# Eight raw weight buffers, two buffers for the modulation's rows, and a root taken in columns

## The chip, the cores and the metric

The kernel runs on one core of a Trainium2 chip. The metric is the device time of one execution, in microseconds (us); before the change it is 2404.76 us, the median of three runs (2402.72 to 2405.74). Lower is better.

The core has engines that run beside each other, each through its own queue of instructions in order: TensorE (PE in the profile; its weight loads are listed as PEld), VectorE (DVE), ScalarE (ACT), GpSimd (POOL) and SyncE (SP). Here SP issues nearly all transfers. Work on data goes on in SBUF, an on-chip memory of 128 partitions; matmuls write to PSUM, a second one.

## The reference

One layer of a decoder trunk over 256 tokens of width 2048, all in float32, and a last norm:

```
mods = (silu(c) @ ada_w + ada_b).reshape(9, 2048)      # modulation: 9 vectors of 2048
h = rms_norm(x, ffn1_norm) * (1 + mods[1]) + mods[0]
x = x + 0.5 * mods[2] * (silu(h @ w_gate) * (h @ w_up)) @ w_down        # first FFN, width 5632
h = rms_norm(x, mix_norm) * (1 + mods[4]) + mods[3]
x = x + mods[5] * mixer(h)      # gated delta rule (8 heads) beside sparse attention (8 heads), gates, w_out
h = rms_norm(x, ffn2_norm) * (1 + mods[7]) + mods[6]
x = x + 0.5 * mods[8] * second_ffn(h)
y = rms_norm(x, final_norm)
```

Nearly all bytes are weights, each read once: 564 MB come from HBM, 151 MB of them the modulation's matrix `ada_w` (2048 x 18432).

## The kernel before, in words

Activations lie transposed: 16 tiles of 128 channels by 256 tokens. A float32 product is made of two parts that TensorE takes in its float32r form: each weight tile is split into a rounded part (`whi`, ScalarE, L186 or L357) and the rest (`wlo`, VectorE, L187 or L358), the activations likewise (`hpair`, `apair`). `product` (L192) runs `whi` against both activation parts (512 columns) and `wlo` against the first (256 columns).

**Weights.** `wload` (L172) fetches a projection's weights in tiles of 512 KB, 4 KB a partition, into buffers of the name `raw`: there are `RB = 6` of them, shared by everything that is loaded under this name. `wsplit` (L181) splits each into one of `WB = 3` pairs of `whi` and `wlo`; a raw buffer is free when `wlo` is written. A projection over 2048 channels (`proj`, L201) has two such tiles and 16 x 2 matmuls, a down-projection of an FFN three tiles and 22 x 2. `block_load` and `block_rows` (L344, L353) do the same for four channel tiles and a gate and up column tile at once.

**Modulation.** The matrix `ada_w` is not multiplied on TensorE. `ada_cols` (L236) loads the 128 rows of one output tile in two halves, each 512 KB, also into `raw` buffers (then called `adaraw`), and VectorE reduces each against `silu(c)` (L248, 1.28 us) into a column of `modc`. A reduction isn't issued at once: it goes to the list `late`, and `behind` (L162) lets it out behind a later `wlo` subtraction, one or two at a time, held to that place in VectorE's order. `ada(n)` (L265) takes n output tiles, two loads each, from a queue; `pace` and `paces` (L332, L545) spread them: 16 over the first 22 projections of the gate and up stage, 32 over the next 42 projections, and in the mixer 4 over 27, 20 over 20 and 24 over 36.

**Order.** The program fixes what depends on what; a planner orders each engine's instructions when the program is built, by its own estimate of when each is ready, and gives buffers out as they come free. On the chip each queue then runs strictly in that order.

**Stages.** The first FFN opens with `start` (L426). The modulation's first two vectors are not there yet, so the first 22 of 44 gate and up tiles are summed in four quarters of the channels, while the rows for the next quarter are loaded and reduced. Before the first quarter, `start` needs the norm's root: 16 matmuls of `ones` against the squares (L432) leave the sum of squares of each token in all 128 partitions, 256 columns wide; the root (`rsqrt`, L273: one start value and three rounds of three VectorE steps) is taken on that tile of 128 x 256, issued when the mods' loop stands at `KT - 5`. After `start` come the other 22 tiles (`gate_up`, L503), with `down(0)` between and `down(1)` after them (L521). Then the mixer: delta rule in four groups of two heads with the compression of keys and values beside it, attention in two groups, the merge (`merge_gates`, L1088, ten tiles ahead of the up-projections), `w_out`; then the second FFN and the last norm.

**Small buffers.** In the mixer each temporary has a name and a number of buffers. The norms after the first one take their root in columns: `token_sums` (L296) makes a 128 x 2 tile, `inv_rms` (L302) takes the root of it and spreads it over the partitions with two matmuls.

Of the kernel before, what the change touches and what calls it, by code (L numbers as in the profile page):

```python
# [18 lines left out]
F32 = mybir.dt.float32  # L19
# [3 lines left out]
AF = mybir.ActivationFunctionType  # L23
OP = mybir.AluOpType
# [3 lines left out]
P = 128  # L28
S = 256
D = 2048  # L30
KT = D // P
FF = 5632
FT = FF // P
NG = 2
GF = FT // NG
AB = 33
H = 8
WB = 3
RB = 6
TB = 6  # L40
MM = 3
NS = 22
SIZES = ((4,), (4,), (4,), (4,))
# [9 lines left out]
EPS = 1e-6  # L53
# [51 lines left out]
def trunk(tc, a, out, stage=99, dbg=None):  # L105
    nc = tc.nc
    ctx = ExitStack()
    with ctx:
# [4 lines left out]

        def ptile(shape=(P, 512), dt=F32, tag="c", bufs=7 - MM):
            return psum.tile(list(shape), dt, tag=tag, name=tag, bufs=bufs)
# [14 lines left out]
        ones = cf[:, C_ONE:C_ONE + P]  # L130
        ident_r = cr[:, 0]
        V = {}
# [101 lines left out]
        ada_q = []  # L234

        def ada_cols(m, d, now=False):  # L236

            part = [V["ada_b"][:, m * KT + d:m * KT + d + 1]]
            for hf in range(2):
                raw = wp.tile([P, HC], F32, tag="raw", name="adaraw", bufs=RB)  # L240
                nc.sync.dma_start(raw, a["ada_w"][m * KT + d, :, hf * HC:(hf + 1) * HC])

                def sums(hf=hf, raw=raw):
                    if hf == 0:
                        out_ = nrm.tile([P, 1], F32, tag="part", name="part", bufs=2)
                    else:
                        out_ = modc[:, m, d:d + 1]
                    nc.vector.tensor_tensor_reduce(out=raw, in0=raw, in1=cact[:, hf * HC:(hf + 1) * HC], scale=1.0,  # L248
                                                   scalar=part[0], op0=OP.mult, op1=OP.add, accum_out=out_)
                    part[0] = out_  # L250

                late.append(sums)
                if now:
                    flush()
                yield
# [170 lines left out]
        def start(fp, n, sizes, wgu, gain):  # L426
            A = nrm.tile([P, KT], F32, tag="A", name="A", bufs=2)
            pt = ptile((P, S))
            for d in range(KT):
                sq = tmp()  # L430
                nc.scalar.activation(sq, xT[:, d], AF.Square)
                nc.tensor.matmul(pt, ones, sq, start=(d == 0), stop=(d == KT - 1))  # L432
            hT = []
            sums = [fp.tile([P, 2, S], F32, tag="a", name="gu", bufs=AB) for _ in range(n - RES)]
            pairs = []
            with tc.tile_pool(name="sp", bufs=1) as sp:
# [41 lines left out]
                for kt, _ in enumerate(mods(*offs[0][0])):  # L478
                    if kt == KT - 5:
                        v = nrm.tile([P, S], F32, tag="ssq", name="vb", bufs=1)  # L480
                        nc.vector.tensor_scalar(v, pt, 1.0 / D, EPS, op0=OP.mult, op1=OP.add)
                        rb = rsqrt(sp, v, "rb")
                for b in range(len(sizes)):
# [13 lines left out]

        def ffn(fp, wgu, wd, m_gate, ticks, first, post=None):
            if True:
# [33 lines left out]

                while len(aT) < AB:
                    aT.append(gate_up(len(aT)))
                down(0)
                while len(aT) < FT:
                    aT.append(gate_up(len(aT)))
                down(1)

# [32 lines left out]
        with tc.tile_pool(name="ffn", bufs=1) as fp:  # L573
            ffn(fp, a["w1gu"], a["w1d"], 2, paces((16 - LT, 2 * (AB - NS)), (32, 42)),
                lambda fp: start(fp, NS, SIZES, a["w1gu"], V["n1"]), post1)
        if stage == 1:
# [9 lines left out]
        with ExitStack() as mx:  # L586
# [14 lines left out]
            def one(tag="q", bufs=12):  # L601
                return mp.tile([P, S], F32, tag=tag, name=tag, bufs=bufs)
# [14 lines left out]

            sm = mp.tile([P, S], F32, name="sm")
            both(win(0), sm)
# [84 lines left out]
            def gdn_group(h0, q, k, v):  # L704
# [113 lines left out]
                for j in range(4):  # L818
                    nc.tensor.transpose(pt[:, j], z[lo, j, lo], ident[lo, lo])
                zq = mp.tile([P, 4, 64], F32, tag="zq", name="zq", bufs=1)  # L820
                nc.scalar.activation(zq[lo], pt, AF.Copy)
# [64 lines left out]
            def gdn_out(h0, oT):  # L886
                for i in range(2):
                    h = h0 + i
                    zg = both(win(W_GZ + h))
                    th = tmp()  # L890
                    nc.scalar.activation(th, zg, AF.Tanh, scale=0.5)
                    sg = mp.tile([P, S], F32, tag="sg", name="sg", bufs=1)
                    nc.vector.scalar_tensor_tensor(sg, th, 1.0, zg, op0=OP.add, op1=OP.mult)
                    sv = sg.rearrange("p (a b) -> p a b", a=2)
                    nc.vector.tensor_mul(sv, sv, v4(oT)[:, :, i])
                    oA[h] = big("oA", 8, (P, 2, S), F32R)
                    split(oA[h], sg)
# [6 lines left out]
            def compress():  # L904
                for b in range(2):
                    cat = mp.tile([P, 2, S], F32, tag="cat", name="cat", bufs=2)
                    for g in range(2):
# [176 lines left out]
            yf = []  # L1084
            mtags = ["kE", "Dt", "N", "o", "vn", "oT", "kd", "kd", "cat", "cat"] + ["pr", "pr", "kk", "kk", "vt", "vt"]
            sgs = []
# [7 lines left out]

            AHEAD = 10
            for d in range(AHEAD):
# [126 lines left out]
```

## Time and profile before

| | |
|---|---|
| median of three runs | 2404.76 us (2402.72 to 2405.74) |
| the profiled execution | 2399.2 us, of which the profile's span is 2397.4 |
| granted TensorE clock, mean | 0.988 of full speed |
| PE, DVE, ACT busy | 96%, 74%, 47% of the span |
| transfers | 571.00 MB, 238 GB/s on the mean |

The page of the profile gives busy time of each engine, the chain of work that ended last (followed back from the last instruction to what released each step), the costliest groups of instructions, and for transfers the time from issue to landing. Other views answer for a stretch: instructions in order of time, busy time and count by windows, the chain in order of time. L187 is line 187 of the kernel. In a row such as `wlo<-raw,whi`, names are those of tiles. Times in a trace start at the span's start.

### The profile page before, as it was taken

The page shows a single profiled execution, that of the slowest core. Times are in us where ns is not written, and L with a number is a line of the kernel's source. Part 1 is how long each engine was busy: PE and PEld are TensorE (multiplying, and loading weights), DVE is VectorE, ACT ScalarE, POOL GpSimd, SP SyncE. Part 2 cuts the span into 40 slices and gives each one's busy share as a digit, 9 for nine tenths or more (in the row PEclk, how much of TensorE's full clock was granted, in tenths as well). Part 3 has the DMA queues.
Part 4 walks back from the last instruction along what each step waited for, and adds up shares of the span by engine and source line. Part 5 has one row for each costly group of instructions (what it writes and reads, how often), then busy time and mean ns, then how long its engine had stood idle before and what let it go on. Part 6 is the DMA issues. An engine that isn't in the chain of part 4 may idle for free.

```text
span 2397.4 us, 38975 instructions
## 1 busy us (share of the span) xinstructions
PE 2301.0 (96%) x15094; PEld 2029.9 (85%) x15094; DVE 1781.4 (74%) x2896; ACT 1133.5 (47%) x1787; POOL 1.4 (0%) x8
## 2 busy tenths in 40 slices
PE   6999999999999999999999999999999999999997
PEld 4999987887778888887778888889888888888886
DVE  6888877777777797778887778879666666555555
ACT  3433544433444474554545444556544444344453
POOL 0000000000000000000000000000000000000000
PEclk8999999999999999999999999999999999999999
DMA  9988678888888745547676888666777777665663
GB/s 320 319 299 301 199 260 286 285 289 286 273 291 268 245 158 188 170 151 249 226 252 214 284 290 283 214 218 216 232 242 243 241 243 219 192 195 189 184 191 123
DMA packets 174493, 571.00 MB, mean 238 GB/s; under 512 B 17890, under 2 KB 18146, under 8 KB 174308
## 3 DMA queue, kind: packets, MB, share of 16 engines
q1 hardware_dynamic: 173584, 566.09, 72.0%
q8 instruction: 118, 1.93, 0.3%
q10 hardware_dynamic: 724, 2.43, 0.3%
q14 instruction: 67, 0.55, 0.1%
HBM read 564.25 MB, written 4.19 MB: 237 GB/s over the span
## 4 chain that ended last, share of the span: by engine, by line
PE 62%; DMA 17%; DVE 12%; ACT 5%; issue 4%; ACTq 0%; DVEq 0%; SPq 0%
PE mm L196 34%; PE mm L198 18%; DMA raw<-in_w1gu_dram 9%; PE mm L363 5%; DVE wlo L187 4%; DMA raw<-in_win_dram 4%; ACT whi L186 3%; DMA raw<-in_w1d_dram 2%; DVE adaraw L248 2%; PE c L363 2%; DVE wlo L358 1%; ACT whi L357 1%; DMA raw<-in_wup_dram 0%; DVE gu L464 0%; PE c L799 0%
## 5 line engine op out<-in xcount | busy, mean ns | idle before, releaser
L196 PE MATMUL mm<-hpair,whi 128*128 128x512 f32 x3536 | 1249.9, 394 | 17.2 <-ACT whi L186 8.9
L187 DVE TENSOR_TENSOR wlo<-raw,whi 128x1024 fp32r<-128x1024 f32 (+1 forms) x666 | 796.5, 1197 | 485.1 <-ACT whi L186 477.0
L186 ACT ACTIVATE whi<-raw 128x1024 fp32r<-128x1024 f32 (+1 forms) x666 | 690.6, 1038 | 800.3 <-PE mm L196 268.3
L198 PE MATMUL mm<-hpair,wlo 128*128 128x256 f32 x3536 | 1009.4, 286 | 20.7 <-DVE wlo L187 20.2
L196 PEld LDWEIGHTS mm<-hpair,whi 128*128 128x128 f32 x3536 | 667.5, 189 | 161.3 <-ACT whi L186 13.3
L198 PEld LDWEIGHTS mm<-hpair,wlo 128*128 128x128 f32 x3536 | 671.7, 190 | 37.4 <-DVE wlo L187 34.8
L196 PE MATMUL mm<-apair,whi 128*128 128x512 f32 x1408 | 490.2, 391 | 0.8 <-ACT whi L186 0.8
L198 PE MATMUL mm<-apair,wlo 128*128 128x256 f32 x1408 | 398.3, 283 | 2.0 <-DVE wlo L187 1.9
L196 PEld LDWEIGHTS mm<-apair,whi 128*128 128x128 f32 x1408 | 265.1, 188 | 56.5 <-ACT whi L186 1.1
L363 PE MATMUL mm<-hpair,whi 128*128 128x256 f32 x1472 | 262.0, 281 | 17.7 <-ACT hpair L323 16.9
L198 PEld LDWEIGHTS mm<-apair,wlo 128*128 128x128 f32 x1408 | 266.8, 190 | 3.7 <-DVE wlo L187 3.6
L363 PEld LDWEIGHTS mm<-hpair,whi 128*128 128x128 f32 x1472 | 226.1, 189 | 18.8 <-ACT hpair L323 17.3
L363 PE MATMUL mm<-hpair,wlo 128*128 128x256 f32 x736 | 208.4, 283 | 6.9 <-DVE wlo L358 6.7
L248 DVE CUSTOM_DVE_ANT_0 adaraw<-adaraw,cact,vec 128x1024 f32<-128x1024 f32 x144 | 184.0, 1278 | 14.0 <-DMA adaraw<-in_ada_w_dram 14.0
L357 ACT ACTIVATE whi<-raw 128x1024 fp32r<-128x1024 f32 x112 | 118.7, 1060 | 155.9 <-DMA raw<-in_w1gu_dram 87.0
L248 DVE CUSTOM_DVE_ANT_0 adaraw<-adaraw,cact,part 128x1024 f32<-128x1024 f32 x144 | 183.9, 1278 | 0.1
L358 DVE TENSOR_TENSOR wlo<-raw,whi 128x1024 fp32r<-128x1024 f32 x112 | 136.3, 1222 | 43.9 <-ACT whi L357 43.5
L363 PEld LDWEIGHTS mm<-hpair,wlo 128*128 128x128 f32 x736 | 138.9, 189 | 10.8 <-DVE wlo L358 10.3
L222 ACT ACTIVATE t<-mm 128x256 f32<-128x256 f32 x237 | 86.7, 367 | 15.5 <-PE mm L198 15.4
L225 DVE TENSOR_TENSOR t<-mm,t 128x256 f32<-128x256 f32 x193 | 80.7, 418 | 4.8 <-ACT t L222 4.7
L529 DVE SCALAR_TENSOR_TENSOR xT<-mm,g,xT 128x256 f32<-128x256 f32 x128 | 61.5, 481 | 7.1 <-PE mm L198 5.4
L514 ACT ACTIVATE t<-t 128x256 f32<-128x256 f32 x63 | 26.0, 413 | 58.2 <-DVE t L225 58.2
(363 smaller groups left out, 1495.4 us busy)
## 6 DMA issues: line engine op xcount, KB each, us to landing
adaraw<-in_ada_w_dram SPq DMA_DIRECT2D x288, 512.0 KB, 5.6
raw<-in_w2gu_dram SPq DMA_DIRECT2D x180, 512.0 KB, 4.7
raw<-in_w1gu_dram SPq DMA_DIRECT2D x176, 512.0 KB, 5.8
raw<-in_win_dram SPq DMA_DIRECT2D x158, 512.0 KB, 4.8
raw<-in_w1d_dram SPq DMA_DIRECT2D x64, 512.0 KB, 5.2
raw<-in_w2d_dram SPq DMA_DIRECT2D x64, 512.0 KB, 3.5
raw<-in_wup_dram SPq DMA_DIRECT2D x32, 512.0 KB, 4.7
raw<-in_wout_dram SPq DMA_DIRECT2D x32, 512.0 KB, 4.6
```

The costliest lines, as they stand in the source:

```text
L186: nc.scalar.activation(hi[:, :n], raw[:, :n], AF.Copy)
L187: behind(nc.vector.tensor_sub(lo[:, :n], raw[:, :n], hi[:, :n]))
L196: nc.tensor.matmul(ps[:, :], hi, pairs[k][:, :, :].rearrange("p a b -> p (a b)"), start=(k == 0), stop=False, skip_group_check=True)
L198: nc.tensor.matmul(ps[:, S:2 * S], lo, pairs[k][:, 0, :], start=False, stop=(k == n - 1), skip_group_check=True)
L222: nc.scalar.activation(t, ps[:, S:2 * S], AF.Copy)
L225: nc.vector.tensor_add(o, ps[:, :S], t)
L248: nc.vector.tensor_tensor_reduce(out=raw, in0=raw, in1=cact[:, hf * HC:(hf + 1) * HC], scale=1.0, scalar=part[0], op0=OP.mult, op1=OP.add, ...
L357: nc.scalar.activation(hi, raw, AF.Copy)
L358: behind(nc.vector.tensor_sub(lo, raw, hi))
L363: nc.tensor.matmul(ps[:, w], l[:, w, k], h[:, r], start=(first and w == k == x == 0), stop=(last and k == kb - 1 and x == 2), skip_group_c ...
L514: nc.scalar.activation(s, g, AF.Silu, bias=bg)
L529: nc.vector.scalar_tensor_tensor(xT[:, d], pd[:, j * S:(j + 1) * S], g05[:, d:d + 1], xT[:, d], op0=OP.mult, op1=OP.add)
```

## The change

`RB` goes from 6 to 8. In the first FFN, once `start` is done, a pool `ring` with `AR = 2` more buffers of the same size is open, and there `ada_cols` takes its buffers from it, so that all eight `raw` buffers go to weights; in `start`, in the mixer and after it the rows still share the `raw` buffers. In `start` the sums of squares are made as columns (the squares are the stationary operand, one column of `ones` the moving one), and the root is taken by `inv_rms`, issued at `KT // 2`, and copied to `rb`. To make room, four temporaries of the mixer take buffers of other names, and the merge's gates lie in other buffers and run eight tiles ahead instead of ten.

```diff
-RB = 6
+RB = 8
 TB = 6
+AR = 2
...
+        own = []
+
+        def ada_tile():
+
+            if own:
+                return own[0].tile([P, HC], F32, tag="ring", name="adaraw", bufs=AR)
+            return wp.tile([P, HC], F32, tag="raw", name="adaraw", bufs=RB)
+
         def ada_cols(m, d, now=False):
...
-                raw = wp.tile([P, HC], F32, tag="raw", name="adaraw", bufs=RB)
+                raw = ada_tile()
...
-            pt = ptile((P, S))
+            pt = ptile()
             for d in range(KT):
                 sq = tmp()
                 nc.scalar.activation(sq, xT[:, d], AF.Square)
-                nc.tensor.matmul(pt, ones, sq, start=(d == 0), stop=(d == KT - 1))
+                for j in range(2):
+                    nc.tensor.matmul(pt[:, j:j + 1], sq[:, j * P:(j + 1) * P], ones[:, 0:1], start=(d == j == 0),
+                                     stop=(d == KT - 1), skip_group_check=True)
...
-                    if kt == KT - 5:
-                        v = nrm.tile([P, S], F32, tag="ssq", name="vb", bufs=1)
-                        nc.vector.tensor_scalar(v, pt, 1.0 / D, EPS, op0=OP.mult, op1=OP.add)
-                        rb = rsqrt(sp, v, "rb")
+                    if kt == KT // 2:
+                        rb = nrm.tile([P, S], F32, tag="ssq", name="rb", bufs=1)
+                        nc.scalar.activation(rb, inv_rms(pt), AF.Copy)
...
-                while len(aT) < AB:
-                    aT.append(gate_up(len(aT)))
-                down(0)
-                while len(aT) < FT:
-                    aT.append(gate_up(len(aT)))
-                down(1)
+                def rest():
+                    while len(aT) < AB:
+                        aT.append(gate_up(len(aT)))
+                    down(0)
+                    while len(aT) < FT:
+                        aT.append(gate_up(len(aT)))
+                    down(1)
+
+                if ring:
+                    with tc.tile_pool(name="ring", bufs=1) as rp:
+                        own.append(rp)
+                        rest()
+                        own.pop()
+                else:
+                    rest()
...
-                lambda fp: start(fp, NS, SIZES, a["w1gu"], V["n1"]), post1)
+                lambda fp: start(fp, NS, SIZES, a["w1gu"], V["n1"]), post1, True)
...
-            sm = mp.tile([P, S], F32, name="sm")
+            sm = one()
...
-                zq = mp.tile([P, 4, 64], F32, tag="zq", name="zq", bufs=1)
+                zq = mp.tile([P, 4, 64], F32, tag="S", name="zq", bufs=1)
...
-                    sg = mp.tile([P, S], F32, tag="sg", name="sg", bufs=1)
+                    sg = mp.tile([P, S], F32, tag="qr", name="sg", bufs=2)
...
-                    cat = mp.tile([P, 2, S], F32, tag="cat", name="cat", bufs=2)
+                    cat = mp.tile([P, 2, S], F32, tag="kk", name="cat", bufs=2)
...
-            mtags = ["kE", "Dt", "N", "o", "vn", "oT", "kd", "kd", "cat", "cat"] + ["pr", "pr", "kk", "kk", "vt", "vt"]
+            mtags = ["kE", "Dt", "N", "o", "vn", "oT", "kd", "kd", "pr", "pr", "kk", "kk", "vt", "vt", "pT", "pT"]
...
-            AHEAD = 10
+            AHEAD = 8
```

More of the change, by code (lines that the diff above doesn't have):

```diff
@@ L495, in start, with ffn @@
             return hT, pairs, ()
-        def ffn(fp, wgu, wd, m_gate, ticks, first, post=None):
+        def ffn(fp, wgu, wd, m_gate, ticks, first, post=None, ring=False):
             if True:
```

## The prediction

> **What bounds the kernel now.** First the page: the busy shares, then the chain that ended last, then the median landing times.
>
> ```profile
> PE 2301.0 (96%) x15094; PEld 2029.9 (85%) x15094; DVE 1781.4 (74%) x2896; ACT 1133.5 (47%) x1787; POOL 1.4 (0%) x8
> ...
> PE 62%; DMA 17%; DVE 12%; ACT 5%; issue 4%; ACTq 0%; DVEq 0%; SPq 0%
> ...
> adaraw<-in_ada_w_dram SPq DMA_DIRECT2D x288, 512.0 KB, 5.6
> ...
> raw<-in_w1gu_dram SPq DMA_DIRECT2D x176, 512.0 KB, 5.8
> ```
>
> PE at 96% looks finished, but matmul ends are modelled and a stretched matmul counts as busy, while 17% of the chain is transfers. So I count matmuls per stretch, in the view by windows.
>
> ```profile
> core 0: us, PE busy (x) PEld busy (x) DVE busy (x) ACT busy (x) POOL busy (x), PEclk, DMA share, GB/s
> 10.00:20.00 10.00, 10.00 (x28) 6.70 (x28) 6.28 (x11) 7.01 (x19) 0.00 (x0) 1.00 1.03 404
> 60.00:240.00 180.00, 171.95 (x1419) 167.27 (x1418) 154.62 (x212) 75.20 (x87) 0.00 (x0) 1.00 0.90 306
> 240.00:300.00 60.00, 60.00 (x517) 60.00 (x516) 49.93 (x77) 35.18 (x62) 0.00 (x0) 1.00 0.62 200
> 300.00:780.00 480.00, 455.86 (x2540) 392.39 (x2540) 361.94 (x518) 202.47 (x273) 0.00 (x0) 0.99 0.84 280
> 1080.00:1320.00 240.00, 225.40 (x1565) 190.81 (x1564) 203.17 (x475) 118.14 (x259) 0.00 (x0) 0.99 0.71 235
> 1320.00:1500.00 180.00, 171.53 (x959) 148.22 (x959) 137.77 (x196) 80.10 (x113) 0.00 (x0) 0.99 0.84 286
> 1740.00:1980.00 240.00, 240.00 (x1387) 212.78 (x1386) 165.01 (x223) 117.07 (x173) 0.00 (x0) 1.00 0.75 243
> ```
>
> The second FFN (1740 to 1980) runs 1387/240 = 5.78 matmuls a us without a hole: a projection of 32 takes 5.54 us. The rest of the first FFN (300 to 780) would make 480 x 5.78 = 2774 and makes 2540: 234 missing, **40.5 us lost**. The merge (1320 to 1500) lacks 81 of 1040, **14.1 us**. The first FFN's opening, in blocks of 256 columns, runs 517/60 = 8.62 when whole; 60 to 240 lacks 132 of 1551, **15.3 us**. The attention stretch (1080 to 1320) has 14.6 us of idle PE. What PE waits for is in the load queue and the chain of waits.
>
> ```profile
> 311.60 4.53 SPq L177 DMA_DIRECT2D raw<-in_w1gu_dram  x4
> 319.01 1.86 SPq L241 DMA_DIRECT2D adaraw<-in_ada_w_dram  x2
> 322.02 1.87 SPq L177 DMA_DIRECT2D raw<-in_w1gu_dram  x2
> 324.70 1.79 SPq L241 DMA_DIRECT2D adaraw<-in_ada_w_dram  x2
> 330.68 1.86 SPq L177 DMA_DIRECT2D raw<-in_w1gu_dram  x2
> 333.69 1.87 SPq L241 DMA_DIRECT2D adaraw<-in_ada_w_dram  x2
> 336.93 0.33 SPq L177 DMA_DIRECT2D raw<-in_w1gu_dram  x1
> ```
> ```profile
> 322.02 6.21 DMA raw<-in_w1gu_dram
> ...
> 328.33 1.07 ACT whi L186
> ...
> 329.43 1.23 DVE wlo L187
> ...
> 330.68 3.79 DMA raw<-in_w1gu_dram
> ```
>
> The loop closes on itself: load 6.21, split 1.07 and 1.23, and only the split's end gives back the buffer for the next load, 8.66 us after the last one (322.02 to 330.68), where PE wants 5.54. A projection with a modulation row takes four of the six buffers. From 311.60 to 336.93 the queue issues 14 tiles for four projections: 25.33 us against 22.2. That is 1.81 us a tile, so each of six buffers turns round in 10.86 us.
>
> **The change, part by part.** *Eight buffers, shared (opening, mixer).* At the same turn-round a tile comes every 10.86/8 = 1.36 us. The mixer's densest stretch, a row at every projection (four tiles), then needs 5.43 us, the merge with 24 rows in 36 projections (3.33 tiles) 4.5: both under 5.54, if the transfers deliver. They did 404 GB/s at 10 to 20 us; the merge at full pace wants 286 x 1040/959 = 310. I take 11 of the merge's 14.1 us (5 to 14), and of the attention's 14.6 idle us, part of which is short dependent work that no buffer shortens, 6 (0 to 12). In the opening VectorE is close behind: 154.62 us busy at 1419 blocks' matmuls is 169 of 180 at 1551. So 5 of 15.3 (0 to 12).
>
> *Two buffers for the modulation's rows (from about 300 us).* Weights alone then have eight buffers at two tiles a projection, four projections deep: their loop is open. The rows get a loop of their own: the reduction ends, the next row half's load is issued, lands, is reduced.
>
> ```profile
> L248 DVE CUSTOM_DVE_ANT_0 adaraw<-adaraw,cact,vec 128x1024 f32<-128x1024 f32 x144 | 184.0, 1278 | 14.0 <-DMA adaraw<-in_ada_w_dram 14.0
> L187 DVE TENSOR_TENSOR wlo<-raw,whi 128x1024 fp32r<-128x1024 f32 (+1 forms) x666 | 796.5, 1197 | 485.1 <-ACT whi L186 477.0
> ...
> L225 DVE TENSOR_TENSOR t<-mm,t 128x256 f32<-128x256 f32 x193 | 80.7, 418 | 4.8 <-ACT t L222 4.7
> ```
>
> 1.28 + 5.6 = 6.9 us against 5.54 where rows follow each other. Each half-row waits in VectorE's order behind a weight subtraction, so a late row holds the next subtraction. `pace` gives runs of three and a pause: two steps of 1.34, 2.7 us late per run. The split may be two tiles ahead (three hi/lo buffers), 5.5 us less its own 1.06 + 1.23: 3.2 us of cover. The pause gives back 5.54 less 2 x 1.23 and two additions of 0.42, 2.2 us. So nearly all is hidden; with that cover gone it is 2.7 us x 11 runs (44 projections), 30 us. The 32 down-projections, longer, give the rows time. I leave a quarter of the 40.5 us for the 0.5 us per run, runs of four and refills: gain 30 (11 to 38). [...]
>
> *The root in columns.* Now the root of a 128x256 tile is woven between the first sixteen reductions, the last three steps after them.
>
> ```profile
> 16.10 1.28 DVE L248 CUSTOM_DVE_ANT_0 adaraw<-adaraw,cact,part 128x1024 f32<-128x1024 f32 x1
> 17.30 0.08 DVE L248 DVE_READ_ACCUMULATOR2_ANT modc<- 128x1 f32 x1
> 17.30 1.28 DVE L248 CUSTOM_DVE_ANT_0 adaraw<-adaraw,cact,part 128x1024 f32<-128x1024 f32 x1
> ...
> 34.42 1.06 ACT L357 ACTIVATE whi<-raw 128x1024 fp32r<-128x1024 f32 x1 [15.06 <-DMA raw<-in_w1gu_dram]
> ...
> 36.81 0.42 DVE L282 SCALAR_TENSOR_TENSOR rby<-rbt,rby 128x256 f32<-128x256 f32 x1
> ...
> 38.44 0.58 PE L363 MATMUL mm<-hpair,whi 128*128 128x256 f32 x1 [16.95 <-ACT hpair L323]
> ```
> ```profile
> 11.51 9.98 PE L432 MATMUL c<-t,cf 128*128 128x256 f32 x32
> ```
> ```profile
> 2384.29 0.61 PE L299 MATMUL c<-cf,ssq 128*128 128x1 f32 x4 [2.00 <-DVE ssq L294]
> ```
> ```profile
> 2384.93 0.16 DVE L305 TENSOR_SCALAR v<-c 128x2 f32<-128x2 f32 x1 [0.70 <-PE c L299]
> ...
> 2386.90 0.16 DVE L282 SCALAR_TENSOR_TENSOR nry<-nrt,nry 128x2 f32<-128x2 f32 x1
> ```
> ```profile
> 2388.37 0.38 ACT L1152 ACTIVATE rb<-c 128x256 f32<-128x256 f32 x1 [4.05 <-PE c L309]
> ```
>
> VectorE has no hole from 16.10 to 37.23. After: fourteen reductions at 1.20 (16.9 us) and eleven narrow steps (2384.93 to 2387.06, 2.1 us) end at 35.1, 2.1 us sooner. The sum matmuls double in number: 32 written are 64 on the engine (two become four in the last norm), 64 x 0.15 = 9.8 us against 9.98, on a PE idle until 38.44. Broadcast and copy (2387.06 to 2388.75, 1.7 us) fall under reductions. PE needs the first split tile too, 34.42 + 1.06 = 35.5. Gain 2 (0 to 5, if the loads also come sooner).
>
> *The rest.* `sm`, `zq`, `sg`, `cat` move into other names' buffers, whose earlier users are a group behind; the gates' lead falls from ten to eight pairs of projections, still 16 x 5.54 = 89 us of PE work over the last head's tail. Nothing, with those 89 us as cover; were it gone, the tail of one head, some us.
>
> **Sum**: 2 + 5 + 30 + 11 + 6 = 54 us. Profiled execution: 2399.2 us, so 2345.2; the median of the runs is 5.6 above it: **2351**. Bounds of the gain: 16 to 81, so 2324 to 2389.
>
> **Rivals.** *A, the wait moves to VectorE.* Rows are late by 2.7 us a run and the cover is used up by other work: the gates, which lose 25.33 - 22.2 = 3.2 a run now, gain 0.5, 5.5 us over 11 runs, and the rest of ffn1 the 5 us that 40.5 - 35 leave it; ffn1 gives 11, in all 35: 2370. For it: 1.34 us a step by the rows' own landing times. Against: 3.2 us of cover.
>
> *B, slower: the load queue stops behind the rows.* SP issues in order; if the next weights stand behind a row that waits for its buffer, the loop is issue 0.33 + 1.54 of the pair, 5.8, 1.06, 1.23, 1.28: 11.2 us for each of some 33 gate projections with rows. Gates: 33 x 11.2, and 11 without rows at their split's 2.3, are 395 us against 44 x 6.33 = 279 now; sixteen down-projections with rows take a third tile, 12.7 against PE's 22/16 x 5.54 = 7.6: 82 more. 198 lost less 24 won elsewhere: 2579. It decides as soon as an issue of weights waits for a reduction. [...] Against: the queue isn't in the order of the program.
>
> ```profile
> 815.76 18.83 SPq L350 DMA_DIRECT2D raw<-in_win_dram  x16
> 834.70 0.36 SPq L571 DMA_DIRECT2D xd<-xT  x1
> ```
>
> The store of the last xT rows comes behind sixteen loads that the program writes after it, so what isn't ready is passed over when the order is planned.
>
> *C, transfers give no more.* If 286 GB/s were all, ffn1 and merge gain nothing: 2 + 5 + 6 = 13, 2392. Against it 306 in the opening, just what ffn1 wants (280 x 2774/2540), and 404. The change would then not do what it says.
>
> *D, all holes close*: 81, 2324.
>
> **How the numbers follow.** Forecast 0.55 (2335 to 2365), A 0.20, D 0.10, C 0.08, B 0.07. The range 2322 to 2390 leaves out B, most of C and the tails. Under 0.2% (4.8 us) is no change: faster 0.86 (a little of C is not), same 0.05, slower 0.09 (B, and planning that goes worse somewhere).
>
> **What would show it.** Right: some 2710 matmuls in 300 to 780; weight loads issued three or four projections ahead; first weight matmul near 36.4; loads nearly gone from the chain. A: idle of the reductions (L248) on row loads, 14.0 us now, grows to 50 or more, and subtractions late. B: SP waiting for `part` and `modc`, weights behind. C: the DMA share at 0.84 with landings far above 5.8. Wrong: the second FFN, without holes now, changing by more than 2 us; or the mixer's dependent stretches longer by the shared names.

## The result, and the profile after

| | before | after |
|---|---|---|
| median of four runs | 2405.03 us (2402.72 to 2405.74) | **2333.81 us** (2329.55 to 2335.14) |
| profiled execution, its span | 2399.2, 2397.4 | 2335.14, 2333.3 |
| granted TensorE clock, mean | 0.988 | 0.998 |

The ratio is **0.9702**, with a 95% interval of 0.9686 to 0.9719: 71 us faster, where the prediction said 54, and inside its range. The two means of the clock don't compare as they stand: they count the time ahead of a trace's first clock record as full speed. That record comes at 17.0 us before and at 49.2 after, and weight loads took about 333 ns until then, against 190 at full clock, as the last section shows. The page of the changed kernel, the parts shown of before (busy shares, chain that ended last, landing times):

```profile
PE 2277.0 (98%) x15130; PEld 2028.2 (87%) x15130; DVE 1777.2 (76%) x2896; ACT 1132.1 (49%) x1788; POOL 1.4 (0%) x8
...
PE 86%; DVE 6%; DMA 4%; issue 2%; ACT 2%; DVEq 0%; ACTq 0%; SPq 0%
...
adaraw<-in_ada_w_dram SPq DMA_DIRECT2D x288, 512.0 KB, 5.8
...
raw<-in_w1gu_dram SPq DMA_DIRECT2D x176, 512.0 KB, 6.0
```

Transfers fell from 17% of the chain to 4%, although a transfer of a row half takes 5.8 us (5.6 before) and one of gate and up weights 6.0 (5.8 before). The view by windows of the changed kernel, columns as in the prediction:

```profile
60.00:240.00 180.00, 178.78 (x1517) 177.72 (x1516) 160.33 (x220) 80.25 (x93) 0.00 (x0) 1.00 0.93 325
...
300.00:780.00 480.00, 475.60 (x2723) 417.77 (x2722) 390.21 (x563) 219.05 (x295) 0.00 (x0) 1.00 0.88 296
1080.00:1320.00 240.00, 233.42 (x1635) 200.35 (x1634) 207.98 (x449) 119.41 (x242) 0.00 (x0) 1.00 0.75 260
1320.00:1500.00 180.00, 180.00 (x1036) 158.81 (x1035) 150.46 (x233) 90.76 (x137) 0.00 (x0) 1.00 0.79 272
1740.00:1980.00 240.00, 240.00 (x1387) 212.74 (x1386) 161.28 (x216) 114.54 (x165) 0.00 (x0) 1.00 0.73 236
```

From 300 to 780 PE makes 2723 matmuls of the 2774 that its own pace allows; it made 2540. The opening lacks 34 of 1551 (132 before), the merge's stretch 4 of 1040 (81 before). The second FFN runs as it did. Now the waits of the two kernels from 297 to 795 us (engine, line and what it waited for: us in all, times, longest); first before, then after:

```profile
ACT whi L186 <- DMA raw<-in_w1gu_dram: 122.4, 55, 5.6
```
```profile
DVE adaraw L257 <- DMA adaraw<-in_ada_w_dram: 34.1, 33, 3.1
...
ACT whi L187 <- DMA raw<-in_w1gu_dram: 6.0, 4, 1.7
```

The split's wait for gate and up weights is nearly gone, 122.4 to 6.0 us. In its place stands a new one, of VectorE for the modulation's rows. (Lines of the changed kernel are counted anew: L186 and L187 are now L187 and L188, the reduction L248 is L257.)

### The profile page after: what moved, and what is told of

It reads as the page before. It is cut to its first block, busy times and chain, and to the rows that moved or that the text cites. A ratio compares the mean times of both kernels' runs of the same rounds, so it can differ in the third digit from the quotient of the medians.

```text
span 2333.3 us, 39052 instructions
## 1 busy us (share of the span) xinstructions
PE 2277.0 (98%) x15130; PEld 2028.2 (87%) x15130; DVE 1777.2 (76%) x2896; ACT 1132.1 (49%) x1788; POOL 1.4 (0%) x8
## 4 chain that ended last, share of the span: by engine, by line
PE 86%; DVE 6%; DMA 4%; issue 2%; ACT 2%; DVEq 0%; ACTq 0%; SPq 0%
PE mm L197 44%; PE mm L199 24%; PE mm L372 11%; DMA adaraw<-in_ada_w_dram 3%; PE c L372 2%; DVE wlo L188 2%; DVE adaraw L257 1%; DMA raw<-in_win_dram 1%; PE c L442 1%; ACT whi L187 1%; DMA raw<-in_w1gu_dram 0%; PE c L1041 0%; ACT junk L741 0%; DVE wlo L367 0%; PE c L818 0%
## 5 line engine op out<-in xcount | busy, mean ns | idle before, releaser
L197 PE MATMUL mm<-hpair,whi 128*128 128x512 f32 x3536 | 1237.5, 392 | 2.0 <-ACT t L219 2.0
L188 DVE TENSOR_TENSOR wlo<-raw,whi 128x1024 fp32r<-128x1024 f32 (+1 forms) x666 | 796.2, 1196 | 393.3 <-ACT whi L187 390.7
L187 ACT ACTIVATE whi<-raw 128x1024 fp32r<-128x1024 f32 (+1 forms) x666 | 690.7, 1038 | 718.3 <-PE mm L197 359.8
L257 DVE CUSTOM_DVE_ANT_0 adaraw<-adaraw,cact,vec 128x1024 f32<-128x1024 f32 x144 | 183.8, 1276 | 34.8 <-DMA adaraw<-in_ada_w_dram 34.8
L257 DVE CUSTOM_DVE_ANT_0 adaraw<-adaraw,cact,part 128x1024 f32<-128x1024 f32 x144 | 183.9, 1278 | 12.8 <-DMA adaraw<-in_ada_w_dram 12.6
L230 ACT ACTIVATE apair<-t 128x256 fp32r<-128x256 f32 x88 | 36.1, 410 | 54.5 <-DVE t L526 48.8
```

The lines of the kernel that those rows point to most:

```text
L187: nc.scalar.activation(hi[:, :n], raw[:, :n], AF.Copy)
L188: behind(nc.vector.tensor_sub(lo[:, :n], raw[:, :n], hi[:, :n]))
L197: nc.tensor.matmul(ps[:, :], hi, pairs[k][:, :, :].rearrange("p a b -> p (a b)"), start=(k == 0), stop=False, skip_group_check=True)
L230: nc.scalar.activation(pair[:, 0], x, AF.Copy)
```

## The experiments

Stage lengths help to compare the kernels. I read them from the traces, as the time between the first matmul of one stage and that of the next, in us. Gates 1 and 2 are the two stages of `gate_up` after `start`, of 22 projections each, which keep PE busy for 22 x 5.54 = 122 us; down 0 is as much work, and down 1 reaches to the mixer's first projection. The mixer stands in three parts: up to the merge's first projection, to the last attention matmul, to `w_out`. From `w_out` on all kernels take the same time within 1 us.

| kernel | first matmul at | opening | gates 1 | down 0 | gates 2 | down 1 | mixer | span |
|---|---|---|---|---|---|---|---|---|
| before | 38.4 | 265.1 | 134.8 | 125.9 | 145.9 | 158.7 | 387.3 + 44.8 + 258.0 | 2397.4 |
| after | 41.4 | 255.4 | 123.3 | 124.3 | 126.3 | 158.1 | 380.3 + 41.3 + 244.3 | 2333.3 |
| eight_only | 41.1 | 255.4 | 122.0 | 122.0 | 122.0 | 157.4 | 377.9 + 41.6 + 244.3 | 2322.4 |
| ring_only | 41.8 | 272.9 | 124.1 | 124.0 | 123.4 | 157.4 | 398.2 + 38.4 + 264.2 | 2383.0 |
| six_four | 41.8 | 268.4 | 122.0 | 122.0 | 122.0 | 157.4 | 397.9 + 38.8 + 265.0 | 2374.3 |
| ring_one | 41.0 | 256.6 | 139.0 | 172.7 | 146.3 | 177.0 | 378.2 + 41.4 + 244.3 | 2435.0 |
| root_wide | 38.3 | 253.8 | 126.1 | 123.2 | 126.6 | 158.1 | 380.8 + 41.4 + 244.3 | 2331.0 |
| root_only | 41.1 | 271.5 | 133.9 | 123.4 | 144.0 | 157.8 | 392.8 + 38.5 + 262.6 | 2404.1 |
| names_only | 37.9 | 268.7 | 134.4 | 125.7 | 142.9 | 158.9 | 392.5 + 38.5 + 263.4 | 2401.4 |
| eight_wide | 37.7 | 254.9 | 122.0 | 122.0 | 122.0 | 157.4 | 381.9 + 41.3 + 244.3 | 2322.0 |
| seven_wide | 37.9 | 255.9 | 122.7 | 124.3 | 125.0 | 157.8 | 383.4 + 44.1 + 244.3 | 2334.2 |
| five_wide | 40.8 | 289.9 | 165.5 | 144.8 | 171.6 | 166.6 | 415.4 + 43.6 + 293.6 | 2570.9 |
| eight_late | 42.2 | 256.4 | 122.0 | 122.0 | 122.0 | 157.4 | 377.0 + 41.3 + 244.3 | 2322.8 |
| eight_moved | 37.8 | 254.3 | 122.0 | 122.0 | 122.0 | 165.6 | 372.4 + 38.8 + 246.9 | 2320.4 |

### Which of the buffers pays: the shared eight, or the rows' own two

**eight_only**: eight shared buffers, and the rows take theirs from them everywhere.

```diff
-                lambda fp: start(fp, NS, SIZES, a["w1gu"], V["n1"]), post1, True)
+                lambda fp: start(fp, NS, SIZES, a["w1gu"], V["n1"]), post1, False)
```

> The changed kernel without the rows' own buffers: eight shared everywhere. Theory (turn-round): 10.86/8 = 1.36 us a tile, four tiles in 5.43 us against PE's 5.54: the first FFN keeps 20 to 30 of its 33 us, time 2337 to 2347. Rival (the rows need buffers of their own, since each holds one from the load until its late reduction): the first FFN keeps half or less, 2350 or above.

**ring_only**: six shared buffers and the rows' own two.

```diff
-RB = 8
+RB = 6
```

> The changed kernel with six raw buffers; the rows' two in the first FFN stay. Theory (a turn-round of 10.86 us shared over the buffers): in the first FFN after its opening six buffers for weights alone are one per 1.81 us where two tiles per 5.54 us are wanted, so that part keeps its whole 33 us; the opening's 9.7 and the mixer's 24.2 us are gone again: about 2334 + 34 = 2368. Rival (eight buffers for weights are needed behind the rows' late reductions): the first FFN keeps half, 2384.

Measured: eight_only 2324.21 us (2323.57 to 2325.57), ratio to before 0.967 [0.9654, 0.9685]; ring_only 2381.65 us (2379.54 to 2384.79), 0.9909 [0.9891, 0.9928]. Both expectations were missed. Ring_only's time lies near its rival's 2384, but not for the rival's reason: the first FFN kept its whole gain (its stages after `start` sum to 528.9 us against 565.3 before), and the loss lies elsewhere, as said below. The shared eight alone do more than the whole change: the median of eight_only lies 9.6 us under the changed kernel's, with ranges that don't touch. The stages after `start` sum to 532.0 us in the changed kernel and to 523.4 here. The rows of the second gate stage, by windows as long as it, first of the changed kernel, then of eight_only:

```profile
544.50:670.80 126.30, 124.04 (x706) 108.06 (x705) 105.87 (x155) 58.81 (x86) 0.00 (x0) 1.00 0.91 315
```
```profile
540.60:662.60 122.00, 122.00 (x707) 108.16 (x706) 107.57 (x159) 59.95 (x86) 0.00 (x0) 1.00 0.93 334
```

The same matmuls (706 and 707 by the windows) take 126.3 and 122.0 us. In 122.0 PE has no hole, and the transfers deliver 334 GB/s. What the rows' own buffers do is seen in the changed kernel in order of time: SP's queue, then VectorE (start, duration, instruction, and in brackets the idle time before it and what ended it), then the chain of waits.

```profile
408.63 0.33 SPq L250 DMA_DIRECT2D adaraw<-in_ada_w_dram  x1
410.08 0.33 SPq L178 DMA_DIRECT2D raw<-in_w1d_dram  x1
411.29 0.33 SPq L250 DMA_DIRECT2D adaraw<-in_ada_w_dram  x1
412.43 0.33 SPq L178 DMA_DIRECT2D raw<-in_w1d_dram  x1
415.76 0.33 SPq L250 DMA_DIRECT2D adaraw<-in_ada_w_dram  x1
417.23 0.33 SPq L178 DMA_DIRECT2D raw<-in_w1d_dram  x1
```
```profile
414.44 1.28 DVE L257 CUSTOM_DVE_ANT_0 adaraw<-adaraw,cact,vec 128x1024 f32<-128x1024 f32 x1 [1.71 <-DMA adaraw<-in_ada_w_dram]
...
415.99 1.22 DVE L188 TENSOR_TENSOR wlo<-raw,whi 128x1024 fp32r<-128x1024 f32 x1
```
```profile
408.63 5.79 DMA adaraw<-in_ada_w_dram
...
418.77 5.64 DMA adaraw<-in_ada_w_dram
...
425.84 0.88 DVE wlo L188
426.76 0.38 PE mm L199
```

A row half is loaded at 408.63, its reduction starts at 414.44 after VectorE stood idle for 1.71 us, and its buffer's next load goes out at 415.76: a turn of 7.13 us. The weight subtraction ordered behind the reduction is late with it, and after the next such load, of 418.77, the chain runs from the row through the subtraction at 425.84 into PE. This is rival A's mechanism. Rival B's first sign came too: SP waits for the row's buffer from 412.76 to 415.76, with a weight load behind it. But that load goes out at 417.23, when the subtraction that frees its own buffer has just ended (415.99 + 1.22 = 417.21), so here the blocked row held no weights back, and B's slow loop did not come about.

**six_four** (six shared buffers, four for the rows) and **ring_one** (eight and one) change the size of the rows' pool.

```diff
-RB = 8
+RB = 6
...
-AR = 2
+AR = 4
```

> Six raw buffers and four for the rows in the first FFN, beside ring_only's six and two; all else as in it. Theory (two row buffers are the bound: 1.28 us of reduction and 5.8 of load come round once per 7.1 us, PE wants 5.54): with four the rows' loop is half as tight and weights keep six, so the stages of the first FFN go from 124.1, 124.0 and 123.4 us to 122.0 each and VectorE's idle on row loads from 41.9 to under 15 us; time 2376 to 2379. Rival (the order in the load queue and not the number is what costs): stages stay at 123.4 or above, time 2380 to 2383.

```diff
-AR = 2
+AR = 1
```

> The changed kernel with one buffer for the rows in the first FFN instead of two. Theory (rows' loop): both halves of a row go one after the other through one buffer, 2 x (1.28 + 4 to 5.8), 10.6 to 14.2 us for each of 48 rows; the stretch from the first gate stage to the last row, 400 us now, takes 510 to 680, and the time is 2440 to 2620. Rival (the wait for rows is taken off by other work): below 2360.

Measured: six_four 2372.87 us (2365.87 to 2376.07), 0.9868 [0.9839, 0.9897]; ring_one 2436.75 us in a single run. Six_four's stages came out as expected, its time 3 us below. Ring_one's time is just under the expected range, and its rows take 590 us from the first gate stage to the last of them, inside it. The waits of the reductions for their rows over the whole execution, in this order: the changed kernel, eight_only, six_four, ring_one.

```profile
DVE adaraw L257 <- DMA adaraw<-in_ada_w_dram: 47.4, 35, 11.3
```
```profile
DVE adaraw L257 <- DMA adaraw<-in_ada_w_dram: 2.1, 1, 2.1
```
```profile
DVE adaraw L257 <- DMA adaraw<-in_ada_w_dram: 2.0, 1, 2.0
```
```profile
DVE adaraw L257 <- DMA adaraw<-in_ada_w_dram: 177.6, 81, 11.0
```

Some 13 us of these waits are the start's in every kernel: VectorE waits 11 us for its first load and 2 for its second, and of eight_only and six_four the view puts the 11 down to another line. With four row buffers, or with the shared eight, nothing else is left, and all three stages run at 122.0; with two, 34.1 us are left, with one 164. So the loss in these stages is the turn of the rows' own loop. It isn't the weights' buffers: six for weights alone (six_four) are enough there, and six_four has as many buffers in all as the changed kernel, ten. Outside these stages six buffers are too few: ring_only and six_four have a mixer of 701 to 702 us where the changed kernel has 666, and even 11 us more than before, with an opening that is 3 to 8 us longer than before. I had carried over only the gain of the middle stages, and had not expected the loss outside. Root_only and names_only, with six buffers too, show part of it (openings of 271.5 and 268.7, mixers of 694); one profile of each doesn't settle where the rest comes from.

### How many shared buffers

The kernel **eight_wide** is eight_only with the root taken on 128 x 256 again (the edit of root_wide, below); **seven_wide** and **five_wide** differ from it in one number.

> Eight shared buffers, no buffers for rows, root on 128x256 as before: the first part of the change alone, with the names that make its room. Theory (the root in columns costs what its undoing gave beside the rows' buffers, 2.7 us, and the rows' buffers 9.6): 2321 to 2322, first block matmul at 38, gate and down stages of the first FFN at 122.0 us each. Rival (the two parts only cost together): 2324 or above.

```diff
-RB = 8
+RB = 7
```

> eight_wide with seven shared raw buffers. Theory (a buffer turns round in 10.86 us): one tile per 1.55 us. The second gate stage has some 77 tiles: 120 us on the mean, and a run of three projections with rows 18.6 against PE's 16.6, covered by the split's 3.2 us: stages of the first FFN at 122 to 126 us. The mixer's stretch with a row at every projection wants 6.2 us where PE needs 5.54 and keeps holes. Time 2325 to 2345. Rival (each buffer gives a like share of the 84 us): half way, 2361, second gate stage at 133.

```diff
-RB = 8
+RB = 5
```

> eight_wide with five shared raw buffers. Theory (10.86 us over five, 2.17 us a tile): second gate stage 77 x 2.17 = 168 us (six: 143 to 146), the last part of the merge likewise longer, the second FFN's stages, two or three tiles in 5.54 or 7.6 us, untouched except where rows run. Time 2480 to 2540. Rival (the turn-round shrinks with fewer transfers under way, since landings get faster): second gate stage below 155 us, time below 2470.

Measured: eight_wide **2319.53 us** (2318.94 to 2323.75), 0.9653 [0.9629, 0.9678], the best kernel here beside eight_moved; seven_wide 2335.22 us (2331.10 to 2338.55), 0.9719 [0.9681, 0.9757]; five_wide 2572.66 us in a single run. Eight_wide came 1.5 us under the expected 2321 to 2322, with stages of 122.0, and seven_wide as expected; five_wide's second gate stage came near the expected 168 us, its time above the expected range. One window, 544 to 700 us, shows what is transferred; before, seven_wide, eight_wide:

```profile
544.00:700.00 156.00, 142.50 (x777) 120.35 (x776) 114.70 (x164) 62.02 (x87) 0.00 (x0) 0.99 0.84 280
```
```profile
544.00:700.00 156.00, 154.35 (x882) 135.34 (x882) 134.81 (x198) 74.31 (x109) 0.00 (x0) 1.00 0.92 321
```
```profile
544.00:700.00 156.00, 156.00 (x902) 138.30 (x901) 136.73 (x203) 76.75 (x111) 0.00 (x0) 1.00 0.93 327
```

The second gate stage loads 44 tiles of weights (22 projections) and, at 32 rows over 42 projections, some 33 halves of rows: 77 tiles. At a turn of 10.86 us, the prediction's number, n buffers need 77 x 10.86/n: 167, 139, 119 and 105 us for n of 5, 6, 7 and 8, where PE needs 122. Measured: 171.6, 145.9, 125.0 and 122.0. In this stage the law holds within 5% while it is the bound, and where law and PE are close (seven) a few us of both remain. For the first gate stage (76 tiles) it reads 138 and 165 us for six and five buffers, where 134.8 and 165.5 were measured; for down 0 (some 72 tiles) it is 3 and 8% long, 130 and 156 against 125.9 and 144.8. Five buffers cost more elsewhere than expected: opening, mixer and down-projections suffer too, and the mean clock falls to 0.968.

### The root in columns

**root_wide** is the changed kernel with the former root; **root_only** is the change without its buffers (six, none of the rows' own).

```diff
-            pt = ptile()
+            pt = ptile((P, S))
...
-                for j in range(2):
-                    nc.tensor.matmul(pt[:, j:j + 1], sq[:, j * P:(j + 1) * P], ones[:, 0:1], start=(d == j == 0),
-                                     stop=(d == KT - 1), skip_group_check=True)
+                nc.tensor.matmul(pt, ones, sq, start=(d == 0), stop=(d == KT - 1))
...
-                    if kt == KT // 2:
-                        rb = nrm.tile([P, S], F32, tag="ssq", name="rb", bufs=1)
-                        nc.scalar.activation(rb, inv_rms(pt), AF.Copy)
+                    if kt == KT - 5:
+                        v = nrm.tile([P, S], F32, tag="ssq", name="vb", bufs=1)
+                        nc.vector.tensor_scalar(v, pt, 1.0 / D, EPS, op0=OP.mult, op1=OP.add)
+                        rb = rsqrt(sp, v, "rb")
```

> The changed kernel with the first root taken on 128x256 again, issued at KT - 5 as before; eight buffers and the rows' two stay. Theory R (the columns cost time: 64 column matmuls last 14.02 us instead of 9.98, and the first narrow step stands in VectorE's order ahead of rows that are already there, 6.11 us of hole): the first block matmul comes near 38 us instead of 41.4 and the time is 2 to 4 us below the changed kernel's. Rival S (the four rows of the next quarter that eight buffers bring forward, 36.61 to 41.41, hold back the first hpair, and the root is innocent): first block matmul at 41 or later, time the same or longer.

> Six raw buffers and no buffers for rows, but the root in columns, the mixer's shared names and the gates' lead of eight. Theory: the root costs 2 to 4 us and the names nothing: 2407 to 2409, first block matmul near 41. Rival 1 (as predicted, 2 us won): 2403, first block matmul near 36.4. Rival 2 (the names or the lead win part of the mixer's 24 us, and not the buffers): 2400 or below.

Measured: root_wide 2331.08 us (2328.56 to 2332.79), 0.9697 [0.968, 0.9714], against 0.9702 with the change: too close to tell. Root_only 2413.24 us (2405.84 to 2420.22), 1.0042 [1.0028, 1.0057], more than expected. What the traces do tell apart is the start. In the changed kernel, PE, VectorE and ScalarE:

```profile
11.59 14.02 PE L442 MATMUL c<-cf,t 128*128 128x1 f32 x64
34.52 1.23 PE L318 MATMUL c<-cf,nry 128*128 128x128 f32 x4 [8.92 <-DVE nry L291]
41.43 0.80 PE L372 MATMUL mm<-hpair,whi 128*128 128x256 f32 x2 [5.68 <-ACT whi L366]
```
```profile
19.45 0.08 DVE L257 DVE_READ_ACCUMULATOR2_ANT part<- 128x1 f32 x1
25.64 0.16 DVE L314 TENSOR_SCALAR v<-c 128x2 f32<-128x2 f32 x1 [6.11 <-PE c L442]
```
```profile
35.79 0.38 ACT L492 ACTIVATE rb<-c 128x256 f32<-128x256 f32 x1 [14.59 <-PE c L318]
...
40.34 1.04 ACT L366 ACTIVATE whi<-raw 128x1024 fp32r<-128x1024 f32 x1
```

In eight_wide, whose root is on 128 x 256, PE and ScalarE:

```profile
11.62 9.07 PE L441 MATMUL c<-t,cf 128*128 128x256 f32 x32
...
37.74 1.23 PE L372 MATMUL mm<-hpair,whi 128*128 128x256 f32 x2 [17.05 <-ACT hpair L332]
```
```profile
32.28 1.06 ACT L366 ACTIVATE whi<-raw 128x1024 fp32r<-128x1024 f32 x1 [13.72 <-DMA raw<-in_w1gu_dram]
```

The sums in columns last until 25.6 instead of 20.7. The narrow step `v` (L314) that needs them stands in VectorE's order ahead of reductions, so VectorE idles for 6.11 us, and all reductions behind it are that much later. The first split of a weight tile is ordered behind `rb` and the first two `hpair` in ScalarE's queue, and comes at 40.34 instead of 32.28. PE starts at 41.4 instead of 37.7.

**eight_late** tries to mend that: eight_only, with the root issued four turns of the loop later.

```diff
-                    if kt == KT // 2:
+                    if kt == KT - 4:
```

> eight_only with the root in columns issued after the twelfth reduction (KT - 4) instead of the eighth. Theory (in the changed kernel VectorE stood 6.11 us before the first narrow step because that step was ordered ahead of rows already there): the hole is filled by reductions, first block matmul at 37 to 39.5 instead of 41.1, time 2320 to 2322, level with eight_wide (2319.5). Rival (the twice as many sum matmuls, 14.02 us, delay the root wherever it stands): 41 and 2324.

Measured: 2324.66 us (2323.77 to 2325.32), 0.9677 [0.9648, 0.9707]; eight_only had 2324.21. VectorE in eight_late:

```profile
26.40 0.16 DVE L314 TENSOR_SCALAR v<-c 128x2 f32<-128x2 f32 x1 [6.98 <-PE c L442]
```

The hole is still there, 6.98 us, and PE starts at 42.2. The expectation was missed, and the rival (the sums delay the root wherever it stands: 41 and 2324) gave the numbers. The place in the program doesn't set the order: the planner does, by its estimate of when the sums are ready, and on the chip they are ready later. That the estimate was too early is read from the hole; what the estimate was isn't in the trace. Why the sums themselves are so slow is told with the prediction below.

### The names and the lead, and rows moved out of the mixer

**names_only**: of the change, only the temporaries' names and the shorter lead of the gates (edits of eight_only and of root_wide, and RB back to 6).

> Six buffers shared, the root on 128x256 as before: only the mixer's shared names and the gates' lead of eight are left of the change. Theory (root_only's 9.6 us over the kernel before come from the root, whose narrow steps change the opening's order, 271.5 against 265.1 us, with some from the mixer): time within 5 us of before, 2402 to 2409, opening at 265, first block matmul at 38.4. Rival (the names and the lead cost): 2409 to 2414, with the mixer's stretches longer than before's by 4 us or more.

Measured: 2403.56 us (2397.09 to 2408.47), 0.9996 [0.998, 1.0012]: no difference that can be told. Root_only differs from it in the root alone, and their ratios to before have intervals that don't touch: with six buffers the root in columns costs some 10 us.

**eight_moved**: eight_wide with eight of the mixer's rows taken earlier, in the down-projections.

```diff
-            ffn(fp, a["w1gu"], a["w1d"], 2, paces((16 - LT, 2 * (AB - NS)), (32, 42)),
+            ffn(fp, a["w1gu"], a["w1d"], 2, paces((16 - LT, 2 * (AB - NS)), (40, 54)),
...
-(20, 20)
+(12, 20)
```

> eight_wide with eight of the modulation's rows moved from the mixer's densest stretch (12 over 20 projections instead of 20 over 20) to the first FFN's last down-projections (40 over 54 instead of 32 over 42). Theory (with eight buffers a row at every projection costs 5.43 us against PE's 5.54, so transfers bound that stretch no more and its holes are dependent work): the mixer up to the merge stays within 3 us of 381.9, time 2317 to 2322. Rival (VectorE's 2 x 1.28 us for each row still lie on the mixer's chain): it is 8 us or more shorter and the time below 2313.

Measured: 2319.56 us (2318.53 to 2322.21), 0.9652 [0.9634, 0.9671], as eight_wide. The time is the expected one, but not for the expected reason: the mixer up to the merge was to stay within 3 us, and it is 9.5 us shorter, as the rival said. The mixer gives 9.5 us up to the merge and 2.5 in the attention, the merge's rest takes 2.6 and the last down-projection, which was free of holes with rows at some of its projections, grows by 8.2. The rows take their cost along, about 1 us a row.

## Why the prediction was right, and where it was not

| step of the prediction | gain said (bounds) | gain measured, profiles before and after |
|---|---|---|
| root, start to the first weight matmul | 2 (0 to 5) | **-3.0** |
| opening | 5 (0 to 12) | 9.7 |
| rest of the first FFN | 30 (11 to 38) | 33.2 |
| attention stretch and what is before it | 6 (0 to 12) | 10.5 (7.0 + 3.5) |
| merge | 11 (5 to 14) | 13.7 |
| second FFN | 0 | 0.0 |
| sum | 54 | 64.1 |
| median over profiled execution | + 5.6 | - 1.3 |

**Right: the turn of a buffer.** 10.86 us for each buffer, read from the load queue of before, explains the gate stages with five, six, seven and eight buffers. Eight are enough, and transfers were no limit: rival C said that 286 GB/s was all, and gates 2 of eight_only ran at 334. That the chain would lose its transfers came true, with weight waits down from 122.4 to 6.0 us. Some 2710 matmuls were announced for 300 to 780; there were 2723.

**Right in kind, and charged rightly as a whole: the rows' loop.** The prediction set 6.9 us for a turn of the rows (7.13 in the row above) and left 10.5 of the 40.5 lost us to it and to refills; by the same count 51 matmuls, 8.8 us, were left. Rival A wanted 50 us or more of idle reductions, and 47.4 came (14.0 before); but of the 34.1 us in these stages PE lost only 8.6 (532.0 less 523.4), a quarter, so the cover of splits made ahead hid the rest, as argued against A.

**Wrong: the reason for those two buffers.** I credited the whole gain of the middle stages to the open loop of the weights, as the change part by part had it (two buffers for the rows). I priced what the shared eight give in the opening and the mixer alone and not in the middle stages, where the same sum would have read 77 x 10.86/8 = 105 us against 122. Without that line it did not come out that the rows' own buffers lose 9.6 us of what eight shared ones give.

**Wrong: the root.** The step that failed is "the sum matmuls double in number ... 64 x 0.15 = 9.8 us against 9.98, on a PE idle until 38.44". They took 14.02 us, 0.22 each. The weight loads (PEld) show the reason. Below are the sums in columns of the changed kernel; then, of before, the wide sums and the sums in columns of the later norms, from which the 0.15 was read (lowest, median and highest ns, times of the first and the last); then two rows of the changed kernel's first block:

```profile
L442 PEld LDWEIGHTS c<-cf,t x64: 287/333/333, 11.6 to 25.2; 128*128 128x128 f32 x64
```
```profile
L432 PEld LDWEIGHTS c<-t,cf x32: 190/190/337, 11.5 to 20.9; 128*128 128x128 f32 x32
L299 PEld LDWEIGHTS c<-cf,ssq x12: 186/190/192, 836.4 to 2384.6; 128*128 128x128 f32 x12
```
```profile
48.69 0.54 PEld L372 LDWEIGHTS mm<-hpair,whi 128*128 128x128 f32 x2
49.99 0.31 PEld L372 LDWEIGHTS mm<-hpair,whi 128*128 128x128 f32 x2
```

The same loads of 128 x 128 take 190 ns in the later norms and 333 here. The trace of before has both paces beside a clock record: from 372.0 us on, at half clock, such loads take 0.33 us, and from 375.4 on, at full clock, 0.19. So I read the 333 as a low clock, though no clock record covers that time. Before, the wide sums begin as slowly, and from 17.0 us on, where the trace's first clock record says full speed, their loads take 190. In the changed kernel that record comes only at 49.2 us, and all loads ahead of it are slow. So the prediction carried a pace at full clock to a place where the loads show a low one. By the later norms' pace (four loads in 0.52 us) the 64 would have taken some 8.3 us; that is an estimate: the changed kernel did not run them at full clock. An idle PE was no cover, since VectorE's next step in order waits for the sums. The first weight matmul came at 41.4, not near 36.4. With the wide root it is at 37.7 to 38.3 in root_wide, names_only, eight_wide, seven_wide and eight_moved (40.8 with five buffers), so the 3 us are shown; what of them is left at the end is 2.7 us between the medians of after and root_wide, no more than their spread, and 4.7 between eight_only and eight_wide. Why it is some 10 us between root_only and names_only is not explained.

**Undersized: opening and mixer.** In the opening I feared VectorE, at 169 of 180 us; it ran 160 at nearly the full count of matmuls. For the mixer, part of the excess may be the clock. The prediction read 0.99 in some windows and gave it no price. In before seven stretches of 3.41 us run at half clock, four of them in the mixer (at 884.0, 1177.5, 1259.5 and 1419.9 us); the changed kernel has none between 49.2 and 2322.5 us of its 2333.3. Half of 3.41 us is 1.7; by the pace of the matmuls in and after the first stretch, in the last section, it is some 1.4. The one at 1419.9 lies in the merge, whose lost time was counted by missing matmuls and so holds it already; the other three make 5.1 us (4.3 by that pace), against 4.5 by which the row of the attention stretch exceeds what was said. That is an estimate by count: no run here had the holes without the clock's steps.

**The offset.** The 5.6 us from the profiled execution to the median were no property of the kernel: in later runs the kernel before lies anywhere from 2396 to 2413 us, and after's profiled run was above its median. That is 7 of the 17 us by which 71 exceeds 54; the other 10 are the terms above.

## What to carry to other kernels

Read the turn of a buffer from the load queue (time from one load into it to the next, here 10.86 us), multiply by the tiles that a stage consumes, divide by the number of buffers, and compare with the compute of that stage: this one line gave the length of the second gate stage with five and six buffers within 5%, and that eight are enough, and it should be worked out for a shared pool before any stream gets buffers of its own. A private pair is a loop of its own, here 7.13 us against a need of 5.54, and its lateness returns through whichever engine handles both streams in order. A step that is cheaper on its own engine can still be dearer: ask which queue holds the instruction that waits for it, and what stands behind it there.

## What the runs showed of the hardware

Between 44.3 and 2385.9 us of before the granted clock stood at half for 3.41 us seven times. By windows, around the first such stretch (columns as in the prediction; the third number from the end is the granted clock):

```profile
368.00:372.00 4.00, 1.21 (x6) 0.58 (x5) 1.60 (x3) 2.25 (x3) 0.00 (x0) 1.00 0.88 325
372.00:375.40 3.40, 3.40 (x12) 2.87 (x11) 3.40 (x4) 1.51 (x3) 0.00 (x0) 0.50 0.68 207
375.40:379.00 3.60, 3.60 (x22) 3.15 (x21) 2.81 (x5) 1.37 (x2) 0.00 (x0) 1.00 0.89 270
```

After 4 us with PE busy for 1.21 us, twelve matmuls take 3.40 us, then 22 take 3.60. Ahead of the seven stretches PE had been idle for 34 to 76% of the last 3.4 us, in holes of 0.7 to 2.5 us. But the 3.4 us from 1471.1 on, with PE idle for 47%, were not followed by half clock, so the share of idle time alone doesn't tell the two apart, and what set the clock down is not shown. At the later pace the twelve matmuls take 1.96 us, so the stretch cost some 1.4 us beside the holes ahead of it; that is an estimate from these windows.

In the changed kernel matmuls on one column followed each other from 12.65 to 25.6 us without a gap, and the first clock record, of full speed, comes at 49.2, well into the first block. Before, with the wide root, it comes at 17.0, in the midst of the sums. Until that record weight loads of 128 x 128 take about 333 ns in both kernels, after it 188 to 190 at full clock. The view by windows shows the time ahead of the first record as 1.00 (24 to 44 us of the changed kernel, for one), so the two means hide a slow start: with that time taken at half clock, an estimate from the length of the loads, before and after have 0.985 and 0.987. Before has a recorded stretch at half clock there, of 20.48 us from 23.8 on, after PE fell idle at the end of the sums, at 21.5; it spans the start of its first block. Why the record comes so much later in the changed kernel is not shown.
